# A stick-breaking layer whose instructions are issued in source order on every engine, with VectorE's part of each step put behind the next step and q's norm factor moved into the sigmoids' scale

## The chip, the cores and the metric

The kernel runs on one core of one Trainium2 chip. The metric is device time in microseconds (us) for one execution of the whole program.

## The reference

The program is a small streaming encoder: 512 tokens of width 1024, two residual layers, all float32. Layer 0 mixes tokens by retention, layer 1 by stick-breaking attention, and each is followed by a SwiGLU block. The change touches only the mixer of layer 1, with 16 heads of 64 channels:

```python
def stick_breaking(h, w_in, q_gain, k_gain, w_o):
    q, k, v = jnp.split(h @ w_in, 3, axis=-1)
    q = rms_norm(heads(q), q_gain)
    k = rms_norm(heads(k), k_gain)
    v = heads(v)
    scale = DH ** -0.5
    for blk in range(S // QB):                 # 4 blocks of 128 queries
        t0 = blk * QB; kend = t0 + QB
        z = jnp.einsum('bhtd,bhsd->bhts', q[:, :, t0:kend], k[:, :, :kend]) * scale
        mask = s_pos[None, :] < t_pos[:, None]
        log_stay = jnp.where(mask, jax.nn.log_sigmoid(-z), 0.0)
        later = lax.cumsum(log_stay, axis=3, reverse=True) - log_stay
        weight = jnp.where(mask, jnp.exp(jax.nn.log_sigmoid(z) + later), 0.0)
        outs.append(jnp.einsum('bhts,bhsd->bhtd', weight, v[:, :, :kend]))
    return o @ w_o
```

The kernel takes the product of sigmoids instead of the sum of their logarithms: a weight is sigmoid(z) times the product of sigmoid(-z) over all later keys.

## The kernel before

The program goes through retention (to about 410 us), SwiGLU block 0 (to about 760), the stick-breaking stage (to about 1035) and SwiGLU block 1. float32 operands are kept as pairs of a high part (suffix h, written by ScalarE, ACT) and a low part (suffix l, the remainder, written by VectorE, DVE), and a product is three matmuls: high by high, high by low, low by high.

The stick-breaking stage is a list of steps, written as strings in `slots` (L1003). Slot n, counted from -1, holds a step for each letter:

- `f`: one weight chunk of a projection, 12 matmuls on a loaded weight `wh`/`wl` that feed PE between the other steps. There are 48 of the input projections of q, k and v for both groups of 8 heads, then 16 of the output projection. Each takes a weight half: its high part `wh` on ACT (L151), its low part `wl` on DVE (L166), its load `raw` on the SP queue (L120).
- `m`, `n` (`sb_ms`, `sb_norm`): a tile's mean square per head (square on ACT L844, sum on DVE L846; at the last of four tiles the power -1/2 of all 32 columns on GpSimd, POOL, L850), and the multiplication of that tile of q or k by the factor `qf` (DVE, L857).
- `q` (`sb_qt`): transposes of q and k for a pair of heads into two PSUM banks (L869), then `kt` (k with its gain) and the two `qs`, as pairs; `kt` is one buffer, and four DMAs on SP (L880) copy its halves into `kk`, which the scores read.
- `Z`, `Y` (`sb_z`): scores of head n for query blocks 0, 1 or 2, 3 (L897 to L899), two sigmoids each (L902, L903), a product scan on DVE (L908) and a multiplication on POOL (L909).
- `w` (`sb_wt`): the weights of head n-1, transposed on PE (L922) in three PSUM banks, then made into pairs `wth`, `wtl` (L254, L255).
- `a` (`sb_av`): the product with v for head n-2 (L943), its two halves added (`o`, L948 and L949), and after each second head the pair `oh`, `ol`.
- `x` loads the residual again, `+` (`sb_add`) adds the output projections that have waited for it.

In this stage the kernel before leaves the order of each engine's instructions to the scheduler of the language: the list of steps is what it starts from, and it moves instructions of ACT, DVE, POOL, SP and PE against one another. The two SwiGLU blocks have `tc.manual_schedule`: what is written is what is issued. A PSUM bank is given out in turn by `psum()` (8 of them), and a step must wait until the last reader of its bank is done.

Of the kernel before, what the change touches and what calls it, by code (L numbers as in the profile page):

```python
# [11 lines left out]
F32 = mybir.dt.float32  # L12
F32R = mybir.dt.float32r
AF = mybir.ActivationFunctionType
# [3 lines left out]
P = 128  # L18
# [3 lines left out]
NT = S // P  # L22
EPS = 1e-6
# [165 lines left out]
def trunk(ctx, tc, x_in, gains_in, ret_tok, ret_ch, ret_o, sb_in, sb_o4, sb_o2, ffn_in2, ffn_in, ffn_out0, ffn_out1, ffn_out2,  # L189
# [11 lines left out]
    turn = [0]  # L201

# [27 lines left out]
    mhalf = cp.tile([P, 8 * NT], F32, name="mhalf")  # L230
# [562 lines left out]
    def sb_open():  # L793
        sb["ctx"] = ExitStack()
        e = sb["ctx"].enter_context
        sb["p"] = e(tc.tile_pool(name="sbp", bufs=1))
        sb["t"] = e(tc.tile_pool(name="sbt", bufs=2))
        mask = st.tile([P, P], F32, tag="sqt", name="mask")
        nc.gpsimd.memset(mask, 0.0)
        nc.gpsimd.affine_select(out=mask, in_=mask, compare_op=ALU.is_gt, fill=-2.0 ** 100,  # L800
                                base=0, pattern=[[-1, P]], channel_multiplier=1)
        for name, src in (("mask", mask), ("ident", ident)):
            sb[name] = sb["p"].tile([P, P], F32R, name=name)
            nc.scalar.activation(sb[name], src, AF.Copy)

    QF, QS, QN, VS, QT, Wt, WT, O = {}, {}, {}, {}, {}, {}, {}, {}

    def sb_chunk(which, g, c, kk):
        def go():
# [10 lines left out]
            for t in range(NT):  # L820
                if which == "v":
# [6 lines left out]
                    to_pair(vs[:, :, 0:SDH], vs[:, :, SDH:P], src, r[:, t : t + 1])  # L828
# [8 lines left out]
            QS[which, g] = st.tile([P, NT, 8], F32, tag="qss", name="qss")  # L837
        return go

    def sb_ms(which, g, t):  # L840

        def go():
            sq = st.tile([P, S], F32, tag="sqt", name="sqt")
            nc.scalar.activation(sq, QN[which, g, t], AF.Square)  # L844
            ss = QS[which, g]
            nc.vector.tensor_reduce(ss[:, t], sq.rearrange("p (h d) -> p h d", d=SDH), AX.X, ALU.add)  # L846
            if t == NT - 1:
                ss = ss.rearrange("p t h -> p (t h)")
                nc.vector.tensor_scalar(ss, ss, 1.0 / SDH, EPS, ALU.mult, ALU.add)
                nc.gpsimd.tensor_tensor(QF[which, g].rearrange("p t h -> p (t h)"), ss, mhalf, ALU.pow)  # L850
# [9 lines left out]
    def sb_qt(p):  # L860


        def go():
# [10 lines left out]
            to_pair(kt[:, 0], kt[:, 1], k, gains[:, 49:50])  # L874
            got = []
            for e in range(2):
                mine, other = HS[e], HS[1 - e]
                kk = sb["t"].tile([P, 2, S], F32R, tag=f"kk{e}", name="kk")
                for half in HS:
                    nc.sync.dma_start(kk[half].bitcast(F32), kt[mine].bitcast(F32))  # L880
                qs = sb["t"].tile([P, S], F32R, tag=f"qs{e}", name="qs")
                to_pair(qs[mine], qs[other], q[mine], gains[mine, 48:49])
# [4 lines left out]
    def sb_z(hd, js):  # L887


        def go():  # L890
            qs, kk = QT[hd // 2][hd % 2]
            both = []
            for j in js:
# [8 lines left out]
                nc.scalar.activation(r[:, :n], bank[:, :n], AF.Sigmoid, scale=-scale)  # L902
                nc.scalar.activation(w, bank[:, :n], AF.Sigmoid, scale=scale)  # L903
                both.append((j, n, w, r))
            for j, n, w, r in both:
# [7 lines left out]
    def sb_wt(hd):  # L913

        def go():
            got = [None] * NT
            for grp in ((0,), (1, 3), (2,)):
# [9 lines left out]
                to_pair(h[:, :at], l[:, :at], bank[:, :at])  # L927
# [8 lines left out]
    def sb_av(hd):  # L936
        def go():
# [10 lines left out]
            nc.scalar.activation(o[HS[e]], bank[HS[1 - e]], AF.Copy)  # L948
            nc.vector.tensor_tensor(o[HS[e]], bank[HS[e]], o[HS[e]], ALU.add)  # L949
            if e == 1:  # L950
# [6 lines left out]
                to_pair(h, l, sb["o"])  # L957
# [39 lines left out]
    for c in range(2):  # L997
# [6 lines left out]
        "ffffffffffmmfmmfnffnffnmnmmmnnnnffffqff",  # L1004
# [16 lines left out]
        "waf",  # L1021
# [3 lines left out]
    todo = {"f": iter(fill), "m": iter(tiles), "n": iter(tiles), "q": iter(range(SH // 2))}  # L1025
    for n, slot in enumerate(slots, -1):
        for what in slot:
            if what == "f":
                fn, ap = next(todo["f"])
                step(fn, *([] if ap is None else [ap]))  # L1030
# [13 lines left out]
    step(lambda: sb["ctx"].close())  # L1044
# [100 lines left out]
```

## Time and profile before

| | us |
|---|---|
| median of the runs shown | 1384.09 |
| lowest run | 1382.78 |
| profiled execution, its own time | 1384.04 |
| span of the profiled execution | 1382.3 |
| PE busy | 1355.9 |
| DVE busy | 887.9 |
| ACT busy | 619.4 |
| POOL busy | 182.9 |

The span is what the profiler's records cover; the profiled execution's own time is 1.74 us more. A third run of 2708.43 us is listed too and is no measure of the kernel. Engines: PE is TensorE, DVE is VectorE, ACT is ScalarE, POOL is GpSimd, SP issues DMAs. "x8" behind a row is a count of instructions. The granted clock is the share of full TensorE speed that the chip granted in a stretch.

### The profile page before, as it was taken

How to read it: one execution, taken by the hardware profiler on the slowest of the kernel's cores; microseconds unless marked ns; L12 is line 12 of the kernel's file. 1: busy time of each engine (PE TensorE's matmuls, PEld its weight loads, DVE VectorE, ACT ScalarE, POOL GpSimd, SP SyncE). 2: the span in 40 equal slices, each digit the busy share in tenths (PEclk: the TensorE clock that was granted, in tenths of full speed). 3: DMA queues.
4: the chain of work that ended last, by engine and by line, in shares of the span. 5: the costliest groups of instructions: out<-in, count | busy, mean ns of one | idle time of the engine just before them, and what ended most of it. 6: DMA issues, size and time to landing. Idle time of an engine off the chain costs nothing.

```text
span 1382.3 us, 19530 instructions
## 1 busy us (share of the span) xinstructions
PE 1355.9 (98%) x7820; PEld 1198.6 (87%) x7820; DVE 887.9 (64%) x1104; ACT 619.4 (45%) x914; POOL 182.9 (13%) x164
## 2 busy tenths in 40 slices
PE   8999999999999999999999999888999999999998
PEld 7888888888889989998998878777879989998997
DVE  6645445345368755774678456689898755774674
ACT  5334233233356533552454356567666533551450
POOL 3000000000131000000002222445351000000000
PEclk9999999999999999999999999999999999999999
DMA  6231322222454654664414245145363654664412
GB/s 229 93 98 62 103 79 85 92 76 83 145 166 110 151 169 125 165 189 129 126 47 167 91 122 138 48 105 149 82 196 110 159 174 123 167 179 126 138 46 92
DMA packets 50602, 170.63 MB, mean 123 GB/s; under 512 B 5968, under 2 KB 6224, under 8 KB 50512
## 3 DMA queue, kind: packets, MB, share of 16 engines
q1 hardware_dynamic: 44752, 148.42, 33.2%
q0 software_dynamic: 5760, 20.97, 8.7%
q8 instruction: 61, 1.00, 0.3%
q14 instruction: 29, 0.24, 0.1%
HBM read 156.79 MB, written 4.19 MB: 116 GB/s over the span
## 4 chain that ended last, share of the span: by engine, by line
PE 92%; DVE 4%; ACT 1%; POOL 1%; issue 1%; DMA 1%; SPq 0%; DVEq 0%; ACTq 0%; POOLq 0%
PE mm L248 19%; PE mm L247 19%; PE mm L249 19%; PE mm L641 10%; PE mm L640 10%; PE mm L638 10%; PE mm L943 1%; PE mm L922 1%; DVE sn L908 1%; POOL qf L850 1%; DVE wl L166 1%; PE mm L899 1%; PE mm L897 1%; PE mm L518 1%; DVE xl L258 0%
## 5 line engine op out<-in xcount | busy, mean ns | idle before, releaser
L151 ACT ACTIVATE wh<-raw 128x1024 fp32r<-128x1024 f32 (+1 forms) x185 | 192.5, 1041 | 356.5 <-PE mm L248 202.8
L166 DVE TENSOR_TENSOR wl<-raw,wh 128x1024 fp32r<-128x1024 f32 (+1 forms) x185 | 229.3, 1242 | 171.6 <-PE mm L248 93.5
L638 PE MATMUL mm<-sxh,wh 128*128 128x256 f32 x640 | 181.3, 283 | 0.0
L641 PE MATMUL mm<-sxh,wl 128*128 128x256 f32 x640 | 181.1, 283 | 0.0
L640 PE MATMUL mm<-sxl,wh 128*128 128x256 f32 x640 | 181.1, 283 | 0.0
L248 PE MATMUL mm<-wl,xh 128*128 128x512 f32 x448 | 176.0, 393 | 2.3 <-DVE wl L166 2.0
L249 PE MATMUL mm<-wh,xl 128*128 128x512 f32 x448 | 175.9, 393 | 0.0
L247 PE MATMUL mm<-wh,xh 128*128 128x512 f32 x448 | 175.7, 394 | 0.1
L248 PE MATMUL mm<-hl,wh 128*128 128x512 f32 (+1 forms) x358 | 138.1, 386 | 0.0
L247 PE MATMUL mm<-hh,wh 128*128 128x512 f32 (+1 forms) x358 | 138.1, 386 | 0.0
L249 PE MATMUL mm<-hh,wl 128*128 128x512 f32 (+1 forms) x358 | 138.0, 385 | 0.0
L640 PE MATMUL mm<-xl,wh 128*128 128x256 f32 x480 | 135.8, 283 | 0.0
L641 PE MATMUL mm<-xh,wl 128*128 128x256 f32 x480 | 135.8, 283 | 0.0
L638 PE MATMUL mm<-xh,wh 128*128 128x256 f32 x480 | 135.8, 283 | 0.0
L640 PEld LDWEIGHTS mm<-sxl,wh 128*128 128x128 f32 x640 | 122.9, 192 | 0.0
L638 PEld LDWEIGHTS mm<-sxh,wh 128*128 128x128 f32 x640 | 122.9, 192 | 0.0
L641 PEld LDWEIGHTS mm<-sxh,wl 128*128 128x128 f32 x640 | 122.9, 192 | 0.0
L248 PEld LDWEIGHTS mm<-wl,xh 128*128 128x128 f32 x448 | 85.0, 190 | 20.4 <-DVE wl L166 2.4
L249 PEld LDWEIGHTS mm<-wh,xl 128*128 128x128 f32 x448 | 84.9, 190 | 17.9
L247 PEld LDWEIGHTS mm<-wh,xh 128*128 128x128 f32 x448 | 84.7, 189 | 17.1 <-ACT wh L163 0.3
L640 PEld LDWEIGHTS mm<-xl,wh 128*128 128x128 f32 x480 | 92.1, 192 | 0.2
L638 PEld LDWEIGHTS mm<-xh,wh 128*128 128x128 f32 x480 | 92.1, 192 | 0.2
(155 smaller groups left out, 2691.2 us busy)
## 6 DMA issues: line engine op xcount, KB each, us to landing
rawg<-in_ffn_in_dram SPq DMA_DIRECT2D x66, 512.0 KB, 4.6
raw<-in_ffn_in_dram SPq DMA_DIRECT2D x42, 512.0 KB, 3.8
raw<-in_ffn_out_dram SPq DMA_DIRECT2D x40, 512.0 KB, 5.5
raw<-in_ret_tok_dram SPq DMA_DIRECT2D x31, 512.0 KB, 3.7
rawg<-in_ffn_in_dram POOLq DMA_DIRECT2D x26, 512.0 KB, 8.3
raw<-in_sb_in_dram SPq DMA_DIRECT2D x24, 512.0 KB, 3.8
raw<-in_ret_ch_dram SPq DMA_DIRECT2D x16, 512.0 KB, 3.7
raw<-in_ret_o_dram SPq DMA_DIRECT2D x16, 512.0 KB, 3.8
```

Source lines behind the costliest of these rows:

```text
L151: self.nc.scalar.activation(h[:, :w], t[:, :w], AF.Copy)
L166: nc.vector.tensor_tensor(l[:, :w], t[:, :w], h[:, :w].bitcast(F32), ALU.subtract)
L247: nc.tensor.matmul(ps, ah, bh, start=start, stop=False)
L248: nc.tensor.matmul(ps, ah, bl, start=False, stop=False)
L249: nc.tensor.matmul(ps, al, bh, start=False, stop=stop)
L518: nc.tensor.transpose(out=bank[:, t * P : (t + 1) * P], in_=OG[h][t][:, b * P : (b + 1) * P], identity=ident)
L638: nc.tensor.matmul(out, h[:, p, s], xh, start=start and p == 0 and s == 0, stop=False, skip_group_check=True)
L640: nc.tensor.matmul(out, h[:, p, s], xl, start=False, stop=False, skip_group_check=True)
L641: nc.tensor.matmul(out, l[:, p, s], xh, start=False, stop=last, skip_group_check=True)
L850: nc.gpsimd.tensor_tensor(QF[which, g].rearrange("p t h -> p (t h)"), ss, mhalf, ALU.pow)
L897: nc.tensor.matmul(bank[:, :n], qs[:, ts], kk[:, 0, :n], start=True, stop=False)
L899: nc.tensor.matmul(bank[:, :n], qs[:, ts], kk[:, 1, :n], start=False, stop=True)
```

## The change

The whole stage, from `sb_open` to the new `sb_close`, is put under `tc.manual_schedule` on all five engines. With it comes a list `delayed`: a step hands the DVE part of its work to `defer`, and `run()` calls it ahead of the next step, or behind the next step where that is one of the first 48 projection steps (`first`). So go the low parts (`pair_later`), the four DMAs into `kk`, the scans with their multiplication on POOL (`sticks`), the sums of squares with the power (`factors`), and the sum and pair of `o` (`gather`). The power is taken per tile (8 columns) instead of per four tiles (32 columns). q is no longer multiplied by its factor: the `n` steps of q are gone from `slots`, POOL makes two scaled copies `qfs` of the factor, and the sigmoids take these as their scale, a pointer instead of a constant. Some steps change place in `slots`, above all `a` ahead of `w` in five of them.

```diff
         for fn in steps:
-            fn()
+            due, delayed[:] = list(delayed), []
+            if getattr(fn, "first", False):
+                fn()
+            for f in due:
+                f()
+            if not getattr(fn, "first", False):
+                fn()
...
     def sb_open():
...
+        sb["order"] = tc.manual_schedule(engines=ALL)
+        sb["order"].__enter__()
...
+    def pair_later(h, l, src, scale=None):
+
+        if scale is None:
+            nc.scalar.activation(h, src, AF.Copy)
+            defer(lambda: nc.vector.tensor_tensor(l, src, h.bitcast(F32), ALU.subtract))
+        else:
+            nc.scalar.activation(h, src, AF.Copy, scale=scale)
+            defer(lambda: nc.vector.scalar_tensor_tensor(l, src, scale, h.bitcast(F32), ALU.mult, ALU.subtract))
...
             nc.scalar.activation(sq, QN[which, g, t], AF.Square)
-            ss = QS[which, g]
-            nc.vector.tensor_reduce(ss[:, t], sq.rearrange("p (h d) -> p h d", d=SDH), AX.X, ALU.add)
-            if t == NT - 1:
-                ss = ss.rearrange("p t h -> p (t h)")
-                nc.vector.tensor_scalar(ss, ss, 1.0 / SDH, EPS, ALU.mult, ALU.add)
-                nc.gpsimd.tensor_tensor(QF[which, g].rearrange("p t h -> p (t h)"), ss, mhalf, ALU.pow)
+            defer(lambda: factors(sq))
+
+        def factors(sq):
+            ss = st.tile([P, 8], F32, tag="qss", name="qss")
+            nc.vector.tensor_reduce(ss, sq.rearrange("p (h d) -> p h d", d=SDH), AX.X, ALU.add)
+            nc.vector.tensor_scalar(ss, ss, 1.0 / SDH, EPS, ALU.mult, ALU.add)
+            nc.gpsimd.tensor_tensor(QF[which, g][:, t], ss, mhalf, ALU.pow)
+            if which == "q":
+
+                for i, sign in enumerate((-scale, scale)):
+                    nc.gpsimd.tensor_scalar(QS[g][:, i, t], QF[which, g][:, t], sign, None, ALU.mult)
...
-            to_pair(kt[:, 0], kt[:, 1], k, gains[:, 49:50])
+            pair_later(kt[:, 0], kt[:, 1], k, gains[:, 49:50])
...
-                for half in HS:
-                    nc.sync.dma_start(kk[half].bitcast(F32), kt[mine].bitcast(F32))
+                defer(lambda kk=kk, mine=mine: [
+                    nc.sync.dma_start(kk[half].bitcast(F32), kt[mine].bitcast(F32)) for half in HS])
...
-                nc.scalar.activation(r[:, :n], bank[:, :n], AF.Sigmoid, scale=-scale)
-                nc.scalar.activation(w, bank[:, :n], AF.Sigmoid, scale=scale)
+                fs = QS[hd // 8][:, :, j, hd % 8 : hd % 8 + 1]
+                nc.scalar.activation(r[:, :n], bank[:, :n], AF.Sigmoid, scale=fs[:, 0])
+                nc.scalar.activation(w, bank[:, :n], AF.Sigmoid, scale=fs[:, 1])
                 both.append((j, n, w, r))
+            defer(lambda: sticks(both))
...
             nc.scalar.activation(o[HS[e]], bank[HS[1 - e]], AF.Copy)
+            defer(lambda: gather(bank, o))
...
     slots = [
-        "ffffffffffmmfmmfnffnffnmnmmmnnnnffffqff",
+        "ffffffffffmmfmmfffffmmmmnnnnffffqff",
         "ZYfff",
         "qZfYqfwf",
         "ffZfaYfmwfm",
         "ZamYfw",
-        "ffZamYfnwf",
-        "ZnfnnqfmwaYmm",
+        "ffZamYfwf",
+        "ZfqfmawYmm",
         "famnZffYfwnnf",
-        "nqYwaZ",
-        "fYqZwa",
-        "YwaxfZf",
+        "nqYawZ",
+        "fYqZaw",
+        "YawxfZf",
         "ZYfawf",
-        "YqwZaf",
+        "YqaZwf",
         "ZfYawfq",
         "+ZaYwff",
         "ZawY",
         "fZYfawf",
-        "waf",
+        "awf",
         "afffff",
     ]
```

How the order moves is shown at three places. First DVE, at the first two pairs of heads. Before, the four low parts of v (`vs`, whose reading frees the PSUM banks of v's projection) stood ahead of the weight's low part `wl`, and scans stood between the parts of the second pair:

```order
L258 SCALAR_TENSOR_TENSOR vs_7154<-mm_6965,rstd_6783,vs_7154 128x8x64
L258 SCALAR_TENSOR_TENSOR vs_7157<-mm_6966,rstd_6783,vs_7157 128x8x64
L258 SCALAR_TENSOR_TENSOR vs_7160<-mm_6967,rstd_6783,vs_7160 128x8x64
L258 SCALAR_TENSOR_TENSOR vs_7163<-mm_6968,rstd_6783,vs_7163 128x8x64
L166 TENSOR_TENSOR wl176_7174<-raw123_7124,wh176_7172 128x1024
L258 SCALAR_TENSOR_TENSOR qs_7204<-mm_7188,gains_76,qs_7204 64x512
```

And after the change:

```order
L167 TENSOR_TENSOR wl176_7195<-raw123_7145,wh176_7193 128x1024
L834 SCALAR_TENSOR_TENSOR vs_7179<-mm_6990,rstd_6785,vs_7179 128x8x64
L834 SCALAR_TENSOR_TENSOR vs_7181<-mm_6991,rstd_6785,vs_7181 128x8x64
L834 SCALAR_TENSOR_TENSOR vs_7183<-mm_6992,rstd_6785,vs_7183 128x8x64
L834 SCALAR_TENSOR_TENSOR vs_7185<-mm_6993,rstd_6785,vs_7185 128x8x64
L834 SCALAR_TENSOR_TENSOR kt_7223<-mm_7218,gains_76,kt_7223 128x512
```

The weight's low part has moved ahead of v's four low parts, and k's low part has come to stand directly behind these.

Second ACT, at the third pair of heads (`kt_7300` after, `kt_7275` before). `wth` are the transposed weights of head 0. Before, `kt` stood behind the two `qs` and two of the three `wth`:

```order
L257 ACTIVATE qs_7281<-mm_7265,gains_76 64x512
L257 ACTIVATE qs_7287<-mm_7265,gains_76 64x512
L254 ACTIVATE wth_7313<-mm_7308 128x512
L254 ACTIVATE wth_7322<-mm_7317 128x512
L257 ACTIVATE kt_7275<-mm_7270,gains_76 128x512
```

After the change it stands ahead of them, with a weight's high part in between:

```order
L833 ACTIVATE kt_7300<-mm_7295,gains_76 128x512
L833 ACTIVATE qs_7303<-mm_7290,gains_76 64x512
L833 ACTIVATE qs_7306<-mm_7290,gains_76 64x512
L152 ACTIVATE wh177_7310<-raw124_7191 128x1024
L830 ACTIVATE wth_7338<-mm_7333 128x512
```

`kt` has moved from the last place to the first of this piece.

Third DVE, at the last head: `o` and `ol` are the last head's output and the low part of its pair, and the `x` are additions of projection results to the residual. Before:

```order
L949 TENSOR_TENSOR o_9165<-mm_9190,o_9165 64x512
L349 TENSOR_TENSOR x3_8365<-mm_9205,x3_8365 128x512
L255 TENSOR_TENSOR ol_9202<-o_9165,oh_9201 128x512
L349 TENSOR_TENSOR x3_8365<-mm_9206,x3_8365 128x512
L166 TENSOR_TENSOR wl194_9227<-raw141_9170,wh194_9225 128x1024
```

And after:

```order
L991 TENSOR_TENSOR o_9188<-mm_9238,o_9188 64x512
L356 TENSOR_TENSOR x3_8413<-mm_9252,x3_8413 128x512
L356 TENSOR_TENSOR x3_8413<-mm_9253,x3_8413 128x512
L831 TENSOR_TENSOR ol_9250<-o_9188,oh_9249 128x512
L167 TENSOR_TENSOR wl194_9275<-raw141_9218,wh194_9273 128x1024
```

`ol` has moved behind both additions of the projection step that was issued ahead of it.

## Rows read from the trace of the kernel before

**Rows 1.** The page: span, and PE's busy time, share and instructions.

```profile
span 1382.3 us, 19530 instructions
PE 1355.9 (98%) x7820; PEld 1198.6 (87%) x7820; DVE 887.9 (64%) x1104; ACT 619.4 (45%) x914; POOL 182.9 (13%) x164
```

**Rows 2.** What PE waited for, 800:1040: waiter, releaser, us in total, times, longest.

```profile
PE mm L922 <- DVE o L949: 4.5, 1, 4.5
PE mm L897 <- DVE o L949: 3.1, 1, 3.1
...
PE mm L247 <- DVE qs L258: 2.4, 1, 2.4
PE mm L897 <- DMA kk<-kt: 1.8, 1, 1.8
```

**Rows 3.** Stretches of 810:1040: length, busy us by engine (PE first), clock, DMA share, GB/s.

```profile
820.00:830.00 10.00, 8.78 (x36) 7.59 (x37) 6.62 (x9) 6.71 (x14) 3.73 (x4) 0.83 0.37 95
...
870.00:880.00 10.00, 6.71 (x27) 5.68 (x28) 8.12 (x9) 3.31 (x6) 4.28 (x3) 0.83 0.00 0
...
910.00:920.00 10.00, 6.86 (x38) 5.68 (x37) 6.20 (x9) 3.14 (x7) 5.49 (x3) 1.00 0.01 2
...
930.00:940.00 10.00, 8.90 (x52) 7.03 (x51) 9.56 (x13) 8.19 (x20) 5.43 (x7) 1.00 0.44 117
...
960.00:970.00 10.00, 7.55 (x47) 6.71 (x46) 9.44 (x14) 7.62 (x17) 3.93 (x4) 0.92 0.60 150
...
sum 230.00, PE 211.57 PEld 178.57 DVE 186.35 ACT 145.38 POOL 94.49; mean PE 9.20 PEld 7.76 DVE 8.10 ACT 6.32 POOL 4.11
```

**Rows 4.** DVE in order of time around 871 us: start, us, instruction, idle before.

```profile
871.82 0.69 DVE L857 TENSOR_TENSOR qn<-qn,qf 128x512 f32<-128x512 f32 x1 [5.97 <-POOL qf L850]
```

**Rows 5.** POOL's instructions by form, whole program: count, busy us, mean ns, idle before.

```profile
L850 POOL TENSOR_TENSOR qf<-qss,mhalf 128x32 f32<-128x32 f32 x4 | 21.7, 5429 | 20.1 <-DVE qss L849 20.1
...
L284 POOL TENSOR_TENSOR rstd<-ms,mhalf 128x4 f32<-128x4 f32 x4 | 4.3, 1066 | 33.0 <-DVE ms L282 33.0
```

**Rows 6.** ACT's instructions by form, 760:1040.

```profile
L151 ACT ACTIVATE wh<-raw 128x1024 fp32r<-128x1024 f32 x32 | 34.1, 1064 | 49.0 <-PE mm L249 43.9 <-PE mm L248 5.0
...
L902 ACT ACTIVATE sn<-mm 128x512 f32<-128x512 f32 x16 | 9.8, 610 | 4.0 <-PE mm L899 3.5 <-POOL w L909 0.6
...
L257 ACT ACTIVATE kt<-mm,gains 128x512 fp32r<-128x512 f32 x8 | 5.5, 688 | 0.8 <-PE mm L869 0.8
```

**Rows 7.** DVE's instructions by form, 760:1040.

```profile
L166 DVE TENSOR_TENSOR wl<-raw,wh 128x1024 fp32r<-128x1024 f32 x32 | 42.3, 1326 | 18.4 <-PE mm L248 15.9 <-PE mm L249 1.2 <-issue 1.2
L255 DVE TENSOR_TENSOR wtl<-mm,wth 128x512 fp32r<-128x512 f32 x32 | 20.8, 684 | 2.2 <-ACT wth L254 1.9
...
L857 DVE TENSOR_TENSOR qn<-qn,qf 128x512 f32<-128x512 f32 x16 | 11.8, 779 | 22.6 <-POOL qf L850 22.6
```

**Rows 8.** PE in order of time: start, us, matmul, count, idle before.

```profile
809.87 1.01 PE L869 MATMUL mm<-ident,qn 128*128 128x128 f32 x6
...
825.51 0.39 PE L247 MATMUL mm<-wh,xh 128*128 128x512 f32 x1
...
830.73 0.39 PE L249 MATMUL mm<-wh,xl 128*128 128x512 f32 x1
...
841.64 0.41 PE L922 MATMUL mm<-ident,w 128*128 128x128 f32 x2 [0.69 <-DVE qs L258]
```

**Rows 9.** The chain that ended last, at the first pair: start, us, piece.

```profile
814.78 0.76 DVE kt L258
815.56 0.53 SPq L880
816.14 4.94 DMA kk<-kt
```

**Rows 10.** SP's issues at the second pair, in order of time.

```profile
833.87 3.15 SPq L880 DMA_DIRECT2D kk<-kt  x4
```

**Rows 11.** ACT at the third pair, in order of time.

```profile
841.84 0.69 ACT L257 ACTIVATE kt<-mm,gains 128x512 fp32r<-128x512 f32 x1
```

More of the change, by code (lines that the diff above doesn't have):

```diff
@@ L22 @@
 NT = S // P
+ALL = {getattr(mybir.EngineType, e) for e in ("PE", "DVE", "Activation", "Pool", "SP")}
 EPS = 1e-6
@@ L201, in trunk, with defer @@
     turn = [0]
+    delayed = []
+    def defer(fn):
+        delayed.append(fn)
     def bank(tag):
@@ L229, in trunk @@
     nc.vector.memset(ones, 1.0)
-    mhalf = cp.tile([P, 8 * NT], F32, name="mhalf")
+    mhalf = cp.tile([P, 8], F32, name="mhalf")
     nc.vector.memset(mhalf, -0.5)
@@ L804, in sb_open, with sb_close @@
             nc.scalar.activation(sb[name], src, AF.Copy)
+    def sb_close():
+        sb["order"].__exit__(None, None, None)
+        sb["ctx"].close()
     QF, QS, QN, VS, QT, Wt, WT, O = {}, {}, {}, {}, {}, {}, {}, {}
+    def pair_later(h, l, src, scale=None):
[5 more added lines that the diff above has]
+            defer(lambda: nc.vector.scalar_tensor_tensor(l, src, scale, h.bitcast(F32), ALU.mult, ALU.subtract))
     def sb_chunk(which, g, c, kk):
@@ L836, in go @@
             QF[which, g] = st.tile([P, NT, 8], F32, tag="qf", name="qf")
-            QS[which, g] = st.tile([P, NT, 8], F32, tag="qss", name="qss")
+            if which == "q":
+                QS[g] = st.tile([P, 2, NT, 8], F32, tag="qs", name="qfs")
         return go
@@ L878, in go @@
                 kk = sb["t"].tile([P, 2, S], F32R, tag=f"kk{e}", name="kk")
-                for half in HS:
-                    nc.sync.dma_start(kk[half].bitcast(F32), kt[mine].bitcast(F32))
+                defer(lambda kk=kk, mine=mine: [
+                    nc.sync.dma_start(kk[half].bitcast(F32), kt[mine].bitcast(F32)) for half in HS])
                 qs = sb["t"].tile([P, S], F32R, tag=f"qs{e}", name="qs")
-                to_pair(qs[mine], qs[other], q[mine], gains[mine, 48:49])
+                pair_later(qs[mine], qs[other], q[mine], gains[mine, 48:49])
                 got.append((qs, kk))
@@ L926, in go @@
                 l = sb["t"].tile([P, at], F32R, tag=f"wtl{grp[0]}", name="wtl", bufs=1)
-                to_pair(h[:, :at], l[:, :at], bank[:, :at])
+                pair_later(h[:, :at], l[:, :at], bank[:, :at])
                 at = 0
@@ L948, in go, with gather @@
             nc.scalar.activation(o[HS[e]], bank[HS[1 - e]], AF.Copy)
+            defer(lambda: gather(bank, o))
+        def gather(bank, o):
+            p, e, g = hd // 2, hd % 2, hd // 8
             nc.vector.tensor_tensor(o[HS[e]], bank[HS[e]], o[HS[e]], ALU.add)
@@ L956, in go @@
                     l = xgp.tile([P, S], F32R, tag="xl", name="ol")
-                to_pair(h, l, sb["o"])
+                pair_later(h, l, o)
                 O[p] = (h, l)
@@ L1024, in trunk @@
     tiles = [(which, g, t) for g in range(2) for which in "qk" for t in range(NT)]
-    todo = {"f": iter(fill), "m": iter(tiles), "n": iter(tiles), "q": iter(range(SH // 2))}
+    proj = [48]
+    todo = {"f": iter(fill), "m": iter(tiles), "n": iter(t for t in tiles if t[0] == "k"), "q": iter(range(SH // 2))}
     for n, slot in enumerate(slots, -1):
@@ L1029, in trunk @@
                 fn, ap = next(todo["f"])
+                fn.first = proj[0] > 0
+                proj[0] -= 1
                 step(fn, *([] if ap is None else [ap]))
@@ L1043, in trunk @@
     assert not any(True for i in todo.values() for _ in i)
-    step(lambda: sb["ctx"].close())
+    step(sb_close)
     s_ffn(1, None, out)
```

4 lines of the change are left out of this document (3 added, 1 removed).

## The prediction

> **What bounds the kernel now.** I read the page first: PE is busy 1355.9 of 1382.3 us [rows 1]. So work taken off the other engines wins little more than PE's idle time, and next I asked where that lies. The stretches put 230 − 211.57 = 18.4 us of it in 810 to 1040 [rows 3], the stick-breaking stage. The view of PE's waits over the same stretch names the long ones: 4.5 us for a transposition of weights (L922) behind `o` on DVE, 3.1 us for scores (L897) behind `o`, 2.4 us for an output projection behind `qs`, 1.8 us for the first scores behind the DMAs into `kk` [rows 2]. The stretches also show what a wait costs beside itself: the granted clock is 1.00 around them, but .83 in 820–830 and 870–880 and .92 in 960–970 [rows 3], so about 1.7, 1.7 and .8 us of full-speed work are lost in those ten-microsecond slices, each right at a wait of PE. The wait at 915 left the clock at 1.00 [rows 3]. PE is thus the bound, with a handful of holes; in 930–940 DVE is nearly full too, 9.56 of 10 us [rows 3], so behind the middle of the stage little room is left on it.
>
> The longest hole is plain in DVE's order of time: DVE sat 5.97 us until POOL's power was done, then ran `qn` and only then `o` [rows 4, 2]. A 128x32 power takes 5.43 us [rows 5], and everything queued on DVE behind the waiting multiplication waits as well.
>
> **What is removed.** The power becomes 16 of 8 columns. No row has that width: 4 columns take 1.07, 32 take 5.43 [rows 5]; on the line between them 8 take 1.07 + 4 × .156 = 1.69 us, between the bounds 1.07 and 5.43 and nearest to the 4. POOL then works 27 instead of 21.7 us on powers, plus 16 small copies, on an engine that is busy 4 to 5.5 us of ten [rows 3]; but no power is long, and for q nothing on DVE waits for it. Eight `qn` of .78 go, 6.2 us of DVE [rows 7], against 12 more short scalings. I count the 4.49 and the 3.14 us as gone, with the 1.7 us of clock at 873: **−9.3 us**. Bounds: 0, if another wait stands there, and −9.3.
>
> **The first scores.** PE reached the transposes of the first pair at 809.87 [rows 8]; eight of them take .87 (six ran in 1.01 with overlap), so they end at 810.75 at the earliest. After the change ACT makes `kt` (.69) and the two `qs` before the weight's high part (1.06) [rows 6]; DVE has that weight's low part (1.33) ahead of `kt`'s [rows 7], which takes .76 [rows 9]. Starts overlap by about .1 each, so `kt` is whole at 810.75 + .6 + .6 + .6 + 1.06 + 1.25 + .75 = 815.6. Before, from the start of the issues at 815.56 the copies took to 816.14 + 4.94 = 821.08 [rows 9]. So the scores start when they did. But the string now puts 24 instead of 32 projection matmuls ahead of them, and 8 of these are 8 × .227 = 1.8 us (23 starts between 825.51 and 830.73) [rows 8]. PE arrives earlier, waits longer and has that work left: **+2.0** (0 if the copies come sooner, 3.3 with one more weight's low part ahead). On SP a load of weights that stood ahead of the copies comes behind them, by an issue of 3.15 us [rows 10]; its weight is needed two projection steps later, so I cost it at nothing, +.4 without that cover.
>
> **The second and third pair.** The weight's low part `wl176` now stands ahead of v's four low parts, and it needs `wh176`, which ACT does behind v's four high parts: 1.06 + 1.33 = 2.4 us [rows 6, 7] come ahead of the freeing of v's banks, which the next transposes need. I take **+2.0** of it (0 to 2.4), since the transposes follow directly.
>
> Then `kt` of pair 3 heads ACT's queue. It has one buffer and must wait until the copies of pair 2 have landed. Before, those were issued at 833.87 [rows 10] and `kt` of pair 3 ran at 841.84 [rows 11], 8.0 us later; then it had stood last in its piece and PE lost .69 [rows 8]. Now, counting from the end of pair 2's transposes: `kt` and its low part 1.6, copies 8.0, `kt` of pair 3 .7, two `qs` 1.3, the low part that frees the third bank of `w` .7: 12.3. PE in that time has Z .7 with .7 of wait, two projection steps of 12 × .227 = 2.7 each, Y 1.1, transposes .9, and .8 of `w`: 9.6. A hole of 2.7 instead of .69: **+2.0** (from −.7, if the copies land in 5 us, to +4.7). I add **+1.7** of clock, as after the waits at 820 and 870 [rows 3]; 0 if it is like 915.
>
> What is queued behind the waiting `kt` is all of ACT: the weight's high part and head 0's `wth`.
>
> At head 1, `wl180` waits for `wh180`, which ACT makes behind the three `wth`, and the three `wtl` follow: .6 + .6 + .4 + 1.06 + 1.33 and two `wtl` of .68 make 6 us [rows 6, 7], less what lies on PE ahead of the scores' bank, a projection step and Z's first block, 3.2, less .6 that runs beside: **+2.3** (0 to 2.8). At pair 5 the last normalised tile of k stands directly ahead of the transposes: **+1.4** (0 to two `qn`, 1.6).
>
> **The middle and the end.** In slots 7 to 9, `a` of a head comes ahead of `w`, and its low parts lie behind a full DVE. Before, PE took 26.2 us there, 2.5 us of it small waits by its gaps (1.10 in 930–940 [rows 3]). DVE's own work after the change is 26.6 us there, by its instructions times their means; with the joins I take 27.8, **+1.6** (−2.5 if all waits vanish, +4.0 if none is covered). In slots 11 to 16 I find five waits, 5.7 us in all: the additions come in a lump at `+` (1.6), and a weight's transposes twice stand close behind their scans (2.2 and 1.1). Away go the 2.4 us at 967 and .8 of clock there [rows 2, 3]: **+2.5** (−3.2 to +2.5). Last, `ol` of the last head stands behind both additions of a projection step, 2 × .68 in the place of one: **+.5** (0 to 1.5).
>
> **The sigmoids.** 128 of them get their scale by a pointer. No sigmoid before has one. A copy with a pointer, `kt`, takes .69, the sigmoid of the same size with a constant .61 [rows 6]: +.08 each, 128 × .08 = 10 us more on ACT. In the stage ACT is busy 3 to 8 us of ten [rows 3], so I cost it at nothing; without that cover it is +10.
>
> The Trainium skill, "ScalarE: Activation LUTs", section "What ACT_TABLE_LOAD costs", says that an activation with immediates takes 186 ns and .833 ns per element and that each pointer operand adds about 93 ns. The trace agrees on both forms (.61 and .69 us at 512 elements). By the page's figure the sigmoids would cost an estimated 12 us of ACT; all of it on the path, it would put the time at 1403.
>
> **The sum.** −9.3 + 2.0 + 2.0 + 2.0 + 1.7 + 2.3 + 1.4 + 1.6 + 2.5 + .5 = +6.7, against 1384.04, the time of the profiled execution itself (its span and 1.74 us), which is the median of the runs shown to .05. That makes 1390.7, and I say **1391**.
>
> **The rivals.** *Not slower.* Copies and low parts arrive in time, since PE always has a projection step of 2.7 us between two steps of a head, and only the first scores wait: 1384.0 − 9.3 − 3.2 + 2.0 = 1373.5. For it: DVE's holes at 866–872 are its only long ones, and the change takes them out. Against it: the copies took 5.5 and up to 8.0 us [rows 9 to 11], two or three projection steps. It decides at the copies of pair 2: if they land within about 5 us of their issue, the hole at `w` of head 0 is gone. All cases from 1362 to 1384 go with it; the floor is PE's idle 18.4 us [rows 3] with 4.2 of clock, which makes 1361.4.
>
> *Clearly slower.* In source order a waiting instruction holds its whole engine. In each of the ten slots 7 to 16 ACT meets both an `o` of `a` and the `wth` of `w` while PE is on its way to them; if each such meeting costs what the largest wait of my walk costs, 1.9 us, these are 38 us where the sum has 12.3, and the time is 1417; with half of that surplus 1404. For it: DVE at 9.56 of ten in 930–940 [rows 3]. Against it: the same list of steps fed the scheduler, so that most of its order is the written one. The Trainium skill, "Perfetto Trace Analysis", section "Tensor Engine Instruction (MATMUL, LD_WEIGHTS)", says that the queues of ACT, DVE and GpSimd are strictly in order; rows 4 agree for DVE, where `o` ran behind the waiting `qn`.
>
> *No effect* (the scheduler's order was the written one) is excluded: the rows of the order differ at the places shown.
>
> **Chances.** Slightly slower, 1384 to 1402: 55%. Not slower, 1362 to 1384: 27%. Clearly slower, 1402 to 1425: 18%. The range leaves out the lowest third of the second case and the upper 60% of the third, 9 and 11 in a hundred: 1369 to 1411; the likeliest case's own range is 1384 to 1402. A measurement of this kernel tells 2%, 27.7 us, from no change: below 1356.4 is under the floor, 1%; above 1411.8 is the far end of the third case, 10%; within, 89%.
>
> **What would show it.** After the change, PE's waits should name no `o` behind a power, and no DVE gap should be as long as 5 us behind `qf`. A wait of some 5 us of the first scores on `kk`, one of L922's counterpart on `qs` of pair 3, and one on `wtl` at head 2's or 3's scores should stand in their place; sigmoids of 512 should take .69 us. I am wrong if the copies land far sooner than 8 us, or if the waits of PE after slot 7 sum to far more than 12 us.

## The result, and the profile after

The changed kernel takes 1409.45 us (median; 1407.15 to 1410.54) against 1384.09 for the kernel before, the middle one of its three runs from 1382.78 to 1385.10 (a fourth, of 2708.43, is no measure of it). The ratio is 1.0183, with an interval of 1.0166 to 1.0199: 25 us slower. The page of the profiled execution, span and PE's busy time:

```profile
span 1405.4 us, 19540 instructions
...
PE 1360.0 (97%) x7820; PEld 1198.6 (85%) x7820; DVE 879.1 (63%) x1108; ACT 628.2 (45%) x914; POOL 192.0 (14%) x192
```

Against [rows 1] the span is 23.1 us longer. PE is busy 4.1 us longer with the same 7820 matmuls, so these ran slower, and it is idle 19.0 us longer. DVE does 8.8 us less, ACT 8.8 more. Neither is near its limit, so the amount of work is an unlikely cause of 23 us; e1_sched below tests it.

What PE waited for, 800:1065 (waiter, releaser, us in total, times, longest):

```profile
PE mm L960 <- DVE qs L834: 9.1, 2, 7.1
PE mm L254 <- DVE x L356: 8.6, 2, 5.9
PE mm L981 <- ACT w L938: 4.4, 3, 2.1
PE mm L931 <- DMA kk<-kt: 4.2, 1, 4.2
PE mm L931 <- DVE wtl L831: 3.3, 3, 1.8
PE mm L981 <- ACT wth L830: 2.0, 1, 2.0
PE mm L903 <- DVE vs L834: 1.5, 1, 1.5
```

The two waits of [rows 2] for `o` behind a power are gone. In their place stand many others, two of them long: 7.1 us of the transposed weights of head 0 behind `qs`, and 5.9 us (with a second of 2.6) at the start of the next SwiGLU block behind `x`, the residual. The kernel before had only one long wait there:

```profile
PE mm L247 <- DVE x L349: 2.6, 1, 2.6
```

The stretches (length, busy us by engine with PE first, clock, DMA share, GB/s), to be read beside [rows 3]:

```profile
840.00:850.00 10.00, 2.87 (x18) 2.35 (x16) 4.36 (x6) 4.08 (x6) 2.03 (x2) 0.81 0.27 79
850.00:860.00 10.00, 10.00 (x41) 8.18 (x41) 2.31 (x4) 1.33 (x2) 0.00 (x0) 0.85 0.80 241
...
930.00:940.00 10.00, 7.67 (x36) 6.92 (x37) 7.49 (x11) 5.95 (x13) 3.96 (x4) 0.83 0.45 106
...
1050.00:1060.00 10.00, 4.09 (x9) 2.79 (x10) 4.81 (x7) 6.69 (x11) 4.81 (x4) 0.55 0.40 134
sum 250.00, PE 211.53 PEld 178.00 DVE 176.42 ACT 155.08 POOL 96.66; mean PE 8.46 PEld 7.12 DVE 7.06 ACT 6.20 POOL 3.87
```

PE idles 250 − 211.53 = 38.5 us in 810 to 1060, where the kernel before idled 18.4 in its 810 to 1040. By the holes between PE's matmuls the difference splits up so: first scores +2.4, transposes of pair 2 +1.5, `w` of head 0 +6.4, scores of head 3 +1.8, transposes of pair 5 +1.2, the two waits behind powers −7.6, slots 7 to 9 +3.3, slots 11 to 17 +4.9, the start of the SwiGLU block +5.9, all others +.2.

The longest hole, in the chain that ended last (start, us, piece):

```profile
836.29 6.39 DMA kk<-kt
842.79 0.69 ACT kt L833
844.05 0.68 ACT qs L833
844.76 1.06 ACT wh L152
845.85 1.24 DVE wl L167
847.11 0.75 DVE kt L834
847.89 0.74 DVE qs L834
848.65 0.77 DVE qs L834
849.55 0.66 PE mm L960 x2
```

`kt` of pair 3 waits for the copies of pair 2 (issued at 834.5), and seven pieces follow in a row, among them a weight's high and low part, until PE goes on.

The end of the stage, on ACT (start, us, instruction, idle before and who ended it):

```profile
1044.97 1.99 ACT L152 ACTIVATE wh<-raw 128x1024 fp32r<-128x1024 f32 x2
1049.55 1.06 ACT L152 ACTIVATE wh<-raw 128x1024 fp32r<-128x1024 f32 x1 [2.58 <-DMA raw<-in_ffn_in_dram]
...
1051.13 0.70 ACT L264 ACTIVATE xh<-x,gains 128x512 fp32r<-128x512 f32 x1
```

A weight's high part waits for its load, and `xh`, the next block's input, stands behind it. This end was in no term of the forecast.

### The profile page after: what moved, and what is told of

It is laid out like the page before. It is cut to its first block, busy times and chain, and to the rows that moved or that the text cites. A ratio compares the mean times of both kernels' runs of the same rounds, so it can differ in the third digit from the quotient of the medians.

```text
span 1405.4 us, 19540 instructions
## 1 busy us (share of the span) xinstructions
PE 1360.0 (97%) x7820; PEld 1198.6 (85%) x7820; DVE 879.1 (63%) x1108; ACT 628.2 (45%) x914; POOL 192.0 (14%) x192
## 5 line engine op out<-in xcount | busy, mean ns | idle before, releaser
L152 ACT ACTIVATE wh<-raw 128x1024 fp32r<-128x1024 f32 (+1 forms) x185 | 192.2, 1040 | 311.3 <-PE mm L255 198.7
L653 PEld LDWEIGHTS mm<-sxl,wh 128*128 128x128 f32 x640 | 120.0, 187 | 0.0
```

Source lines behind the costliest of these rows:

```text
L152: self.nc.scalar.activation(h[:, :w], t[:, :w], AF.Copy)
L653: nc.tensor.matmul(out, h[:, p, s], xl, start=False, stop=False, skip_group_check=True)
```

## Experiments

Three theories were set against each other. *Order*: source order costs the time, through instructions that wait at the head of an engine's queue. *Deferral*: DVE's parts come too late. *Work*: the pointers and POOL's extra instructions cost it. Times are medians of three rounds; each ratio is to runs of the kernel before on the same chip (1383.2 to 1385.0).

| run | what it is | us | ratio, interval |
|---|---|---|---|
| e1_sched | changed, scheduler's order | 1369.8 | .9891 (.9876–.9906) |
| e2_tail | changed, scheduler's order at the end | 1400.9 | 1.0115 (1.0100–1.0130) |
| e3_qlater | changed, pair 3 later | 1407.9 | 1.0161 (1.0142–1.0180) |
| e4_qfactor | before, q's factor in the sigmoids | 1384.2 | .9996 (.9981–1.0010) |
| e5_nodefer | changed, nothing deferred | 1397.7 | 1.0102 (1.0082–1.0122) |
| e6_const | changed, constant scales | 1405.4 | 1.0156 (1.0134–1.0178) |
| e7_ahead | changed, always deferred ahead of the next step | 1395.7 | 1.0086 (1.0069–1.0104) |
| e8_schednodefer | scheduler's order, nothing deferred | 1367.6 | .9886 (.9863–.9909) |
| e9_oldslots | e8 with the old list | 1370.7 | .9913 (.9893–.9934) |
| e10_aheadtail | e7 and e2 | 1388.6 | 1.0036 (1.0023–1.0049) |
| e11_addsfirst | changed, additions first | 1410.0 | 1.0196 (1.0178–1.0214) |
| e12_pow32 | e4 with the new list | 1380.6 | .9977 (.9961–.9994) |
| e13_wfirst | e10, `w` ahead of `a` again | 1391.8 | 1.0048 (1.0032–1.0065) |
| e14_pow8 | before, powers of 8 columns | 1370.4 | .9893 (.9876–.9910) |
| e15_manual | before, manual order | 1412.5 | 1.0199 (1.0177–1.0221) |

### The order alone, both ways

e1_sched takes the manual order out of the changed kernel, e15_manual puts it alone into the kernel before:

```diff
-        sb["order"] = tc.manual_schedule(engines=ALL)
-        sb["order"].__enter__()
...
-        sb["order"].__exit__(None, None, None)
```

> The changed kernel with its manual order of the stage taken out: deferred calls, q's factor in the sigmoids, powers of 8 columns and the new list of steps stay, and the scheduler orders the instructions. Theory 'order' (the 25 us came from instructions that wait at the head of an engine's queue): the two long holes of the changed kernel (7.13 us ahead of the third bank of w, 5.93 and 2.64 us at the start of the last SwiGLU block) shrink to what the kernel before had (.69 and 2.57), the clock comes back, and the time is 1375 to 1390. Rival 'work' (the pointers of the sigmoids and POOL's extra instructions cost it): ACT and POOL have the same work as in the changed kernel, and the time stays over 1400.

> The kernel before with one part alone: the stage in manual order, with the old list of steps, no deferral, powers of 32 columns and q normalised. Theory 'order' (source order by itself costs some 27 us, as e5_nodefer, 1397.7, against e8_schednodefer, 1367.6): 1384 + 27 and what the long powers hold up in an order that can't go around them, 1411 to 1440. Rival (source order is harmful only with the new list or the deferral): 1380 to 1395.

Measured: 1369.8 and 1412.5. Taking the order out wins 40 us, more than the theory's 1375 to 1390 allowed, and makes the kernel 1% faster than before; putting it in alone costs 27 us. ACT works the same 628.2 us in e1_sched as in the changed kernel, and POOL 199.8 instead of 192.0, so the rival *work* is out as the cause of the 25 us. The page of e1_sched:

```profile
PE 1349.5 (99%) x7820; PEld 1188.6 (87%) x7820; DVE 884.2 (65%) x1108; ACT 628.2 (46%) x914; POOL 199.8 (15%) x192
```

What PE waits for in e15_manual:

```profile
PE mm L248 <- DVE x L350: 10.8, 2, 8.1
...
PE mm L925 <- DVE qs L259: 3.0, 1, 3.0
```

The hole at the end and the one behind `qs` are there without deferral, new list or pointers.

### The parts that were to bring the gain

e4_qfactor is the kernel before with q's factor in the sigmoids; e14_pow8 the kernel before with short powers:

```diff
-            ss = QS[which, g]
-            nc.vector.tensor_reduce(ss[:, t], sq.rearrange("p (h d) -> p h d", d=SDH), AX.X, ALU.add)
-            if t == NT - 1:
...
-                nc.gpsimd.tensor_tensor(QF[which, g].rearrange("p t h -> p (t h)"), ss, mhalf, ALU.pow)
+            ss = st.tile([P, 8], F32, tag="qss", name="qss")
+            nc.vector.tensor_reduce(ss, sq.rearrange("p (h d) -> p h d", d=SDH), AX.X, ALU.add)
+            nc.vector.tensor_scalar(ss, ss, 1.0 / SDH, EPS, ALU.mult, ALU.add)
+            nc.gpsimd.tensor_tensor(QF[which, g][:, t], ss, mhalf, ALU.pow)
```

> The kernel before with one part of the change alone: q is not normalised, its factor (power of 32 columns, as before) goes into the sigmoids' scale by a pointer; the scheduler orders the stage from the old list of steps. Theory 'a power on the path' (PE's hole of 4.49 us at 873 came from DVE's wait for q's power): that hole goes with 1.7 us of clock, the one of 3.14 us at 915 (k's power) stays: 1377 to 1380. Rival 'pointers' (128 times .08 us more on ACT reaches the path): 1384 to 1394.

> The kernel before with one part alone: the power per tile of 8 columns, 16 instead of 4; q is still normalised on DVE, constants in the sigmoids, the scheduler's order, the old list. With e4_qfactor (1384.2, q's factor alone) and e9_oldslots (1370.7, both) it tells what q's factor adds to the short powers. Theory 'short powers carry it': both holes that ended behind a 5.43 us power (4.5 and 3.1 us) go with some clock, 1370 to 1375. Rival 'both are needed' (q's multiplication still waits on DVE ahead of o): 1377 to 1383.

> The kernel with the manual order taken out (e1_sched, 1369.8), and with each deferred call made at once as well. It asks whether the gain over the kernel before came from the written order too. Theory (the scheduler finds its own order, the gain comes from the short powers and q's missing multiplication): 1368 to 1373. Rival (the scheduler starts from the written order, and the deferred one is the better start): 1376 to 1384.

> The kernel with the scheduler's order and no deferral (e8_schednodefer, 1367.6), with the old list of steps. So against the kernel before it has q's factor in the sigmoids and the powers of 8 columns, and nothing else. Theory 'short powers' (what e4_qfactor lacked is that k's powers of 5.43 us stay): the hole of 3.1 us at 915 goes, DVE gets its multiplications sooner, 1367 to 1374. Rival 'list' (the new list of steps gave the gain): 1379 to 1384.

> The kernel with q's factor in the sigmoids and the scheduler's order (e4_qfactor, 1384.2), with powers of 32 columns as there and the new list of steps. Theory 'short powers': k's power still holds DVE for 5.43 us and PE for about 3, 1378 to 1385. Rival 'list': 1366 to 1373.

Under the scheduler's order this makes a table: without either part 1384, q's factor alone 1384.2, short powers alone 1370.4, both 1370.7. q's factor is worth nothing, with the short powers or without; these are the gain. e4_qfactor was a miss: the hole of 4.49 us did go, but the first scores started 7.9 us after the issue of the copies into `kk` instead of 5.7 (in both kernels two loads of weights stood right ahead of the copies, so what made them slower is not shown), the hole of the first scores grew from 1.8 to 4.0 us, and PE was busy 1359.0 instead of 1355.9 us. The new list has a median some 3 us lower under either kind of power (1370.7 to 1367.6, 1384.2 to 1380.6), but the intervals of each pair overlap, so a gain from it is not shown. Deferral adds nothing there (1369.8 with, 1367.6 without). e8_schednodefer has the lowest median and is faster than both kernels; e1_sched, e9_oldslots and e14_pow8 can't be told from it.

The page of e14_pow8, what PE waits for in it, and a stretch of it:

```profile
span 1369.3 us, 19563 instructions
...
PE 1349.0 (99%) x7820; PEld 1190.0 (87%) x7820; DVE 890.6 (65%) x1116; ACT 618.0 (45%) x914; POOL 190.9 (14%) x176
```

```profile
PE mm L247 <- DVE x L349: 2.6, 1, 2.6
PE mm L247 <- DVE qs L258: 2.4, 1, 2.4
```

```profile
950.00:960.00 10.00, 7.56 (x50) 6.79 (x49) 9.60 (x14) 7.62 (x17) 3.92 (x4) 1.00 0.58 149
```

No wait behind `o` is left. The wait of 2.4 us for `qs` is the one of [rows 2], but the clock around it stays at 1.00, where it was .92 [rows 3].

### Deferral

e5_nodefer makes each deferred call at once; e7_ahead keeps deferral but always puts it ahead of the next step:

```diff
-        delayed.append(fn)
+        fn()
```

```diff
-                fn.first = proj[0] > 0
+                fn.first = False
```

> The changed kernel (manual order) with each deferred call made at once: VectorE's part stands directly behind ACT's part of its step, and the copies into kk are issued before the two qs are made. Theory 'in-order queues' (what costs is that instructions wait at the head of a queue, and putting DVE's part behind the next step was meant to soften that): DVE now waits for each step's sigmoids and high parts before it does the next weight's low part, so the holes of the middle grow by some 10 us: 1412 to 1430. Rival 'deferral' (the late DVE parts are what costs 25 us): the time falls below 1400.

> The changed kernel with the deferred part always ahead of the next step, also where that is a projection step (so a weight's low part no longer stands ahead of v's, k's, q's and w's low parts). Theory 'weight parts in the way' (at w of head 0 a weight's high part of 1.06 and low part of 1.24 us stood ahead of the low parts that free its bank, at the scores of head 3 likewise): the holes of 7.13, 1.81 and 1.50 us shrink by about 2.3, 1.8 and 1.5: 1402 to 1405. Rival (the weight's low part is then late for its own projection step): new holes at the projections, 1408 to 1415.

Measured: 1397.7 and 1395.7. For e5_nodefer the rival was right and my theory wrong: deferral as written costs 12 us in source order. e7_ahead, faster than its theory's 1402 to 1405, says where: at the projection steps, behind which the deferred part is put. What PE waits for in e7_ahead:

```profile
PE mm L254 <- DVE x L356: 8.3, 2, 5.6
PE mm L960 <- DVE qs L834: 4.9, 2, 2.9
...
PE mm L931 <- DMA kk<-kt: 0.8, 1, 0.8
```

The first scores wait .8 instead of 4.2 us, `w` of head 0 2.9 instead of 7.1, and the waits of 1.5 for `vs` and 1.8 for `wtl` are gone. No new wait for a weight's low part came up. So 3.4 + 4.2 + 1.5 + 1.8 = 10.9 us of holes, and the clock with them, came from deferred parts that stood behind a projection step, and so behind a weight's low part and the high part that it waits for. The edit moves all of a step's deferred work, the issue of the copies too (829.4 instead of 834.5 for pair 2), and no run moves the weight's parts alone.

### The hole at head 0

e3_qlater moves the transposes of pair 3:

```diff
-        "qZfYqfwf",
+        "qZfYfwqf",
```

> The changed kernel with one letter moved: in slot 1 the transposes of pair 3 come behind the transposed weights of head 0 and a projection step, not ahead of them. Theory 'k waits at the head of ACT's queue' (kt of pair 3 waits for the copies of pair 2, and behind it stand the parts that free w's third bank): the hole of 7.13 us is gone, and about 1.7 us of clock with it: 1400 to 1403, if nothing takes its place. Rival (the copies are late for whoever comes next, so that the hole moves by a step): 1406 to 1410.

Measured: 1407.9, not to be told from the changed kernel's. The hole of 7.13 us is gone, but 2.40 came up ahead of the moved transposes, and the hole at the end grew from 5.93 to 8.16:

```profile
PE mm L254 <- DVE x L356: 10.8, 2, 8.2
...
PE mm L903 <- DVE wtl L831: 2.4, 1, 2.4
```

The rival's time was right, but its late copies are not what the new hole waits for: that is a low part of `w` on DVE. What made the hole at the end longer, the next section shows.

### The end of the stage

e2_tail ends the manual order ahead of the last four projection steps. e11_addsfirst keeps it, and writes a step's two additions ahead of its high and low parts:

```diff
-        for a in sb["add"]:
-            add_x(*a)
+        for m, bank, _ in sb["add"]:
+            add_x(m, bank, None)
+        for m, _, gcol in sb["add"]:
+            if gcol is not None:
+                norm_in(m, gcol)
```

> The changed kernel, with its manual order ended ahead of the last four output-projection steps, so that their additions to the residual and the pairs of the next block's input are left to the scheduler. Theory 'addition, high part, low part in turn' (in source order DVE does one addition, waits for ACT's high part, does the low part and only then the next addition, 2.15 us for each tile instead of 1.3): the holes of 5.93 and 2.64 us fall to about 2.6 in all, 6 us of idle time go and 2 to 3 us of clock with them: 1400 to 1403. Rival (the weight's load, for which ACT waited 2.58 us, holds the input back): the holes stay, and the time is within 2 us of 1409.5.

> The changed kernel with one rule of its end altered: the additions of a projection step's two tiles are written ahead of the high and low parts of both, still in manual order, so that ACT's queue at the end has the same order and DVE's has not. It splits what e2_tail won (8.5 us). Theory 'in turn' (DVE's addition, ACT's high part, DVE's low part one after another): the holes of 5.93 and 2.64 us fall by 4 or more, 1402 to 1405. Rival 'load ahead of the high parts' (ACT's queue waits 2.6 us for a weight's load and the input's high parts stand behind it): the hole of 5.93 stays, 1406 to 1410.

> The two edits e7_ahead (deferred parts always ahead of the next step, 13.7 us) and e2_tail (manual order ended ahead of the last four projection steps, 8.5 us) together, on the changed kernel. Theory (two separate places): the gains add, 1409.5 - 13.7 - 8.5 = 1387, so 1385 to 1390. Rival (the holes at the end come from weight loads that are late in absolute time, so that time won earlier is lost there): 1392 to 1396.

Measured: 1400.9, 1410.0 and 1388.6. e2_tail came as expected, but e11_addsfirst shows that the reason given for it is not enough. With the additions in front there is one hole of 9.18 us instead of two of 5.93 and 2.64. PE and ACT of e11_addsfirst there:

```profile
1062.70 0.79 PE L254 MATMUL mm<-xh,wh 128*128 128x512 f32 x1 [9.18 <-DVE x L356]
```

```profile
1057.02 1.06 ACT L152 ACTIVATE wh<-raw 128x1024 fp32r<-128x1024 f32 x1 [6.51 <-DMA raw<-in_ffn_in_dram]
1057.98 0.71 ACT L264 ACTIVATE xh<-x,gains 128x512 fp32r<-128x512 f32 x1
```

ACT waited 6.51 us for a load, and the last four `xh` stood behind. DVE there:

```profile
1050.74 1.28 DVE L356 TENSOR_TENSOR x<-mm,x 128x512 f32<-128x512 f32 x2
```

The inputs of two of these `xh` were ready at 1052.0; the additions for the other two stood on DVE behind the low parts of the first. In e2_tail the scheduler has put that weight behind all of them, as it had in the kernel before (last `xh` at 1033.29, weight at 1034.44):

```profile
1051.51 0.73 ACT L264 ACTIVATE xh<-x,gains 128x512 fp32r<-128x512 f32 x1 [0.52 <-DVE x L356]
...
1052.66 1.04 ACT L152 ACTIVATE wh<-raw 128x1024 fp32r<-128x1024 f32 x1
```

So theory *load ahead of the high parts* is what the traces show, though no run moves that weight alone. The load itself, from its issue to its landing, in the chains of the changed kernel, e11_addsfirst, e3_qlater and e7_ahead (start, us, piece):

```profile
1036.78 12.69 DMA raw<-in_ffn_in_dram
```

```profile
1042.32 14.62 DMA raw<-in_ffn_in_dram
```

```profile
1032.99 14.92 DMA raw<-in_ffn_in_dram
```

```profile
1024.68 12.35 DMA raw<-in_ffn_in_dram
```

It is issued when a `wl` on DVE has freed its buffer, behind six other loads on SP; one of the same size (512 KB) that was issued ahead of the six, at 1030.4 in the changed kernel, landed after 3.6 us. In e3_qlater it took 2.2 us longer than in the changed kernel, and by that the hole at the end is longer. In e11_addsfirst it took 1.9 us longer while the holes there grew by .6 in all, so what the additions are worth by themselves stays open. Why the load took longer in these runs is not shown. Time won earlier need not be lost here, as the rival of e10_aheadtail had it: e7_ahead won 13.7 us earlier, its load took 12.35 us and its hole was 5.6. e10_aheadtail has nearly both gains (13.7 + 8.5 us by the single runs, 20.9 measured).

### The pointers, and the moved letters

e6_const gives the sigmoids constants again (q's factor is computed but left out of the scores). e13_wfirst puts `w` ahead of `a` again in e10_aheadtail.

> The changed kernel with constant scales in the sigmoids: q's factor is computed as before but left out of the scores. It prices the pointers by themselves. Theory (ACT has cover): sigmoids of 512 fall from about .70 to .61, ACT has about 10 us less, and the time moves by less than 4 us, 1405 to 1410. Rival 'pointers on the path': the holes of PE that end with a sigmoid (4.4 us before the product with v, .6 before scores) go and the clock with them, 1395 to 1402.

> The kernel e10_aheadtail (manual order with the two edits, 1388.6), with the transposed weights ahead of the product with v again in slots 7, 8, 9 and 11, as in the old list. In e10 the product waits 1.9 to 2.1 us for the sigmoids of the scores right ahead of it. Theory 'the order of the queue, not this pair' (whichever comes first needs the next bank, and this is freed by sigmoids that stand in ACT's queue behind kt and both qs): the holes of the middle move to the transposes and the time stays within 3 us, 1386 to 1391. Rival 'the moved letters' (a ahead of w makes the holes): 1380 to 1385.

Measured: 1405.4 and 1391.8. A sigmoid of 512 in the changed kernel and in e6_const (mean ns of one behind the busy time):

```profile
L937 ACT ACTIVATE sn<-mm,qfs 128x512 f32<-128x512 f32 x16 | 11.1, 696 | 0.1
```

```profile
L937 ACT ACTIVATE sn<-mm 128x512 f32<-128x512 f32 x16 | 9.8, 610 | 0.3 <-PE mm L933 0.2
```

A pointer costs .086 us, as the .08 of the prediction. The Trainium skill, "ScalarE: Activation LUTs", section "What ACT_TABLE_LOAD costs", states about 93 ns for each pointer operand; the trace agrees nearly. ACT works 10 us less in e6_const. Its time is 4 us lower than the changed kernel's, but the intervals overlap (1.0134 to 1.0178 and 1.0166 to 1.0199), so that the pointers reach the path in source order is not shown. In the scheduler's order they cost no more than the multiplications that they replace save (e9_oldslots 1370.7 against e14_pow8 1370.4). In e13_wfirst the holes of 2.1 and 1.9 us ahead of `a` are there ahead of `w`, and one of 2.9 us is new: it is not the letters. The time is just above the theory's range and can't be told from that of e10_aheadtail. What the holes wait for, on PE and ACT of e10_aheadtail:

```profile
917.31 0.80 PE L980 MATMUL mm<-wth,vs 128*128 128x512 f32 x1 [2.07 <-ACT w L937]
```

```profile
914.24 0.69 ACT L832 ACTIVATE kt<-mm,gains 128x512 fp32r<-128x512 f32 x1 [3.42 <-PE mm L902]
914.82 1.36 ACT L832 ACTIVATE qs<-mm,gains 64x512 fp32r<-64x512 f32 x2
...
916.69 0.57 ACT L937 ACTIVATE w<-mm,qfs 128x384 f32<-128x384 f32 x1
```

PE waits until the second sigmoid of 384 is done (917.26); `kt` and both `qs`, for which PE is not waiting then, stand ahead of it on ACT. No run moves these. e10_aheadtail is still 19 us above e1_sched, and how that divides among the waits of the middle is not shown.

## Why the prediction was right and wrong

The forecast was 1391, slightly slower. The time, 1409.45, lies near the upper end of the range, in the third case, *clearly slower*, which had 18%. The sign was right, the size not: +25 us where the sum had +6.7. Two steps failed above all. The path was followed only to `ol`, so the start of the next SwiGLU block, which costs 5.9 us of idle time, was in no term. And the chain at the third pair left out the weight's parts and two low parts on DVE, so a hole of 7.13 us was put at 2.7. That the time still lies within the range is owed to the width of its third case, not to these steps.

- **What is removed.** Right in place, too small in size. Both waits behind powers are gone, and e14_pow8 prices the short powers at −14.6 us (1385.0 to 1370.4) where the sum had −9.3. PE's idle time fell by 6.1 there, its busy time by 6.9 (1349.0), so the clock gave back far more than the one dip of 1.7 us that I had counted. A power of 8 columns takes 1.84 us, not 1.69. That q's missing multiplication is worth something was wrong: it is worth nothing.
- **The first scores, the second pair, head 3, pair 5.** Right: a hole of 4.17 us with the idle time up by 2.4 (sum +2.0); 1.50 (+2.0); 1.81 (+2.3); 1.15 (+1.4). The cause of the first three was as said, a weight's parts ahead of `kt`, `vs` and `wtl`; in e7_ahead these holes are gone or below 1 us. Pair 5 waits for `qn` there too. At head 3 my sum was wrong: its pieces make 5.35 us, not 6, so by its own rows the term was +1.6.
- **The third pair.** The step was right, its term not: a hole of 7.13 us, not 2.7, with 6.4 us more idle time than before, beyond the bound of +4.7 too. The copies took 8.2 us, near my 8.0, but by luck: in the kernel before they had landed at 840.7, 6.8 us after their issue, and `kt` ran later because `wth` stood ahead of it on ACT. What I left out of the chain were the weight's high part (1.06) and low part (1.24), `kt`'s low part (.75) and the first `qs`'s (.74), 3.8 us. The row of the order with `wh177` between `qs` and `wth` stood in front of me; the sentence on what is queued behind `kt` named it, and the sum did not have it.
- **The middle.** Slots 7 to 9: +3.3 us of holes and a clock of .83 in two slices, where I had +1.6 in all. Slots 11 to 17: 7.4 us of holes against 2.45 before. I had 5.7 and .5 there, which is near, but took .8 us of clock off for the dip of before, where the changed kernel has slices of .83 at 970 and 1020.
- **The end of the stage.** The step failed that followed the path only to `ol`. Behind it come the additions, `xh` and `xl` of the next block, inside the manual order, and no term had them. They cost 5.9 us of idle time and a clock of .55 in 1050–1060; e2_tail gives 8.5 us back. My own sign of being wrong came true only by this: the holes from slot 7 on sum to 13.2 us without the start of the SwiGLU block and to 21.8 with it.
- **The sigmoids.** Costed at nothing; that they cost more is not shown (e6_const).
- **The rivals.** *Clearly slower* named the mechanism that decided, a waiting instruction that holds its whole engine, but put it at `o` and `wth` of slots 7 to 16. Its argument against, that the same list fed the scheduler and most of the order is the written one, was the wrong one: the places where the scheduler departs from it are worth 27 us alone (e15_manual) and 40 in the changed kernel (e1_sched). Its 1417 is 1416 by its own numbers (1390.7 + 38 − 12.3), and the 12.3 is not added up anywhere. *Not slower* had DVE's holes right: without the order the change makes 1369.8 (e1_sched).

The view of [rows 3] has two more slices below 1.00, which I passed over when I counted the clock:

```profile
970.00:980.00 10.00, 10.00 (x54) 8.69 (x53) 6.80 (x10) 6.07 (x14) 2.97 (x4) 0.91 0.19 61
...
1030.00:1040.00 10.00, 7.43 (x29) 5.81 (x29) 8.68 (x9) 6.18 (x10) 7.29 (x5) 0.83 0.69 187
```

All five slices together lose 6.8 us of full-speed work. In e14_pow8 every slice from 800 to 1030 shows 1.00, which fits the 6.9 us by which PE is busy less there.

A step by step sum from runs: before 1384; manual order alone 1412.5; with short powers, q's factor and the new list 1397.7 (e5_nodefer); with deferral behind projection steps 1409.5.

Not settled is why PE's clock stayed at 1.00 in e14_pow8 beside the wait of 2.4 us, where it fell in the kernel before. That the holes ahead of it were shorter (1.3 us at most from 820 on) is one difference among several.

## What to carry to other kernels

Source order is no neutral choice: each instruction that waits for a transfer or another engine holds everything written behind it on its engine, so follow each queue past the end of the edited stage, up to the first matmuls of the next one, before a sum is made. When a chain is walked through a queue, every instruction in the rows of the order counts, also those of another purpose (here a weight's high and low part, 1.06 + 1.24 us). And take an edit of several parts apart first: one of them, the power per tile, was worth 14 us alone, and the order hid it.

## What the runs showed of the hardware

- A power on GpSimd takes 5.43 us for 128x32 and 1.84 for 128x8, so four short ones take 1.9 us more than a long one, and still win, since the first result is there 3.6 us sooner. In the changed kernel:

```profile
L880 POOL TENSOR_TENSOR qf<-qss,mhalf 128x8 f32<-128x8 f32 x16 | 29.3, 1840 | 23.1 <-DVE qss L879 23.1
```

- The same hole did not always cost clock: 2.4 us beside .92 in the kernel before, beside 1.00 in e14_pow8. Of the 13.0 us by which that kernel's span is shorter (1369.3 against 1382.3), 6.9 are matmuls that ran faster.
- Around a hole of 7.1 us of PE the granted clock was .81 and .85 in two slices of ten, around holes of 5.9 and 2.6 us it was .55 in one.
- The Trainium skill, "Perfetto Trace Analysis", section "Tensor Engine Instruction (MATMUL, LD_WEIGHTS)", states that the queues of ACT, DVE and GpSimd are strictly in order. The trace agrees: in e11_addsfirst an `xh` whose input was ready at 1052.0 ran at 1057.98, behind a weight's high part that waited for its load.
